# A two-layer decoder trunk on one core: more weight chunks in seven block products, and later stores of the residual

## The chip, the cores and the metric

The kernel runs on one core of one Trainium2 chip. The metric is the device time of one execution in microseconds (us), lower is better. Before the change the median of three executions is 2463.84 us (2461.32 to 2466.27).

The engines are named as in the profile: PE is TensorE's matmul, PEld its loading of the stationary operand, DVE is VectorE, ACT is ScalarE, POOL is GpSimd, SP is SyncE, which here only issues DMAs.

## The reference

Input and output are float32, 256 positions by 2048 channels, two layers. Cut to what matters:

```python
for l in range(2):
    h = rms_norm(x, mix_norm[l])
    proj = h @ w_in[l]                       # 2048 x 7680: q, k, v, u, v of the gating unit, two gates
    branch_a = sliding_window_attention(...) @ w_attn_branch[l]     # 1024 x 2048
    branch_b = chunked_sgu(...) @ w_sgu_branch[l]                   # 1024 x 2048
    x = x + (sigmoid(gate_a) * branch_a + sigmoid(gate_b) * branch_b) @ w_out[l]      # 2048 x 2048
    h2 = rms_norm(x, ffn_norm[l])
    x = x + (silu(h2 @ w_gate[l]) * (h2 @ w_up[l])) @ w_down[l]     # 2048 x 5632 twice, 5632 x 2048
```

All weights are float32 and are read from HBM once.

## The kernel before

**Split products.** A float32 product is made of three matmuls (lines 399 to 401): every operand is split into a high part and the rest, and high by high, high by low and low by high are summed in PSUM. For a weight piece of 128 partitions by 1024 elements ACT makes the high part (`whi`, line 256) and DVE the rest (`wlo`, line 264). The activations are kept in "units": 512 channels, transposed, split into `uh` and `ul`.

**Jobs and parts.** The work is a list of jobs; a job is one product of all units with 1024 columns of a weight (a pair of 512-column chunks; `g6` stands below for the gate columns of the pair of chunks 6 and 7, `u6` for the up columns of that pair, `d0` and `d2` for the two column halves of the down projection). A unit of a job is either *whole*, in four parts of 12 matmuls each (48 matmuls, 4 weight pieces to split), or in *seven products* (the 2 by 2 block scheme that saves one block product of eight): 42 matmuls, but 7 pieces to split and 4 block sums more, which DVE makes out of the raw weights (line 240: `sum<-raw`, `raw<-raw,raw`, `raw<-raw,sum`, `sum<-raw,raw`). Each of these DVE instructions works on 128 x 1024 elements. The number of units of a job in seven products is its `m`; they stand at the job's head, and the tail of their products is mixed with the whole parts behind them. For seven products the units need sums of their own activations too (`sh`, `sl`); for these the first two units of the gate and up jobs have them already, since the gate jobs have `m` = 2.

**What sets the order.** Everything is in a fixed order, written by the program: no engine is scheduled freely. `Stream` runs ahead of PE: the low parts up to five pieces ahead (`N_LOW` = 5 buffers), the high parts six, the raw weights in five buffers of 1 MB (`N_RAW`). A block sum is emitted at a place counted in parts from the head of its job (`SUM_AT`): for `m` = 2 five to six of the eight stand among the last parts of the job before, since DVE works ahead. Loads go out on SP's queue, in order, each when DVE has split the last piece of the buffer that it takes. `tick` counts slots, 0.5 for a product and 1 for a whole part; `after(n, fn)` puts work n slots later. After each job its accumulators are evicted: ACT for gate columns (`silu`, line 1088), DVE for up columns (line 1094) and for the residual (lines 995 and 997).

**Transposing.** A new unit is transposed in blocks: DVE transposes 32 x 32 blocks (`blk`, line 483), sixteen small DMAs issued by POOL bring them into place (`tt`, line 489), ACT scales (line 583, where there is a norm) and splits (`uh`, lines 511 and 587), DVE makes the rest (`ul`, lines 508 and 590). A unit with sums has DVE make and ACT split these as well (lines 520, 523, 508).

**The residual.** It lies in HBM (`kept0` to `kept3`, 512 KB each) between its uses. `fetch_x` (line 356) brings a quarter in, `added` adds the accumulators, and `keep_x` (line 359) stores it, 7 or 8 slots after the end of its column chunk, on SP's queue. This happens behind the output projection (where the quarters also become the units of the next norm, and so are transposed while the first gate job `g0` runs) and behind each of the three rounds of the feed-forward part.

**Rounds.** The 11 chunks of the feed-forward part go in three rounds (0 to 3, 4 to 7, 8 to 10): gate pair, up pair, gate pair, up pair, then the down projection of these chunks. Chunk 10 has no partner; its gate and up columns form one job, `gu10`.

```python
M_OUT, M_FFN, M_DOWN = (0, 1), (2, 1, 1), 1
...
                    for w, m in zip((w_gate, w_up), M_FFN if f else (1, 1)):
```

So before the change every gate pair but the first has two units of four in seven products, every other job of the feed-forward part one.

Of the kernel before, what the change touches and what calls it, by code (L numbers as in the profile page):

```python
# [37 lines left out]
N_BIG = 25  # L38
G_BUSY, G_LAND = 3.5, 3
T1_LATE, THEN_LATE, UNIT_LATE = (1.5, 3), (3, 7), (3, 3)  # L40
Q_FIRST = 15
Q_STEP = 4
LOAD_BY = (1, 2, 3, 4)
ROUNDS = ((0, 1, 2, 3), (4, 5, 6, 7), (8, 9, 10))
M_OUT, M_FFN, M_DOWN = (0, 1), (2, 1, 1), 1
M_Q = 0
M_GATE, M_ATT, M_SGU = (1, 1, 1, 1), (0, 0), (1, 0)
M_V, M_U = 1, 1
# [4 lines left out]
def hybrid_trunk(ctx: ExitStack, tc: tile.TileContext, x, mix_norm, w_in, q_norm, k_norm, sinks,  # L53
# [106 lines left out]
    for l in range(DEPTH):  # L160
        wl = w_in[l]
        for o in (0, None)[::-1 if l == 0 else 1]:
            add_job([wl[:, o:o + CW2]], m=M_Q * l) if o is not None else add_job([wl[:, O_KV:O_KV + CW]])
        for o, m in ((O_V, M_V), (O_U, M_U), (O_GATE, M_GATE[0]), (O_GATE + CW2, M_GATE[1])):
            add_job([wl[:, o:o + CW2]], m=m)
        add_job([wl[:, O_GATE + D:O_GATE + D + CW2]], m=M_GATE[2])
        for i, o in enumerate((0, CW2)):
            add_job([w_attn_branch[l, :, o:o + CW2]], m=M_ATT[i])
        add_job([wl[:, O_GATE + D + CW2:O_GATE + 2 * D]], m=M_GATE[3])
        for i, o in enumerate((0, CW2)):  # L170
            add_job([w_sgu_branch[l, :, o:o + CW2]], m=M_SGU[i])
        for i, o in enumerate((0, CW2)):
            add_job([w_out[l, :, o:o + CW2]], m=M_OUT[i])
        for fs in ROUNDS:
            for f in fs[::2]:
                if f + 1 < NF:
                    for w, m in zip((w_gate, w_up), M_FFN if f else (1, 1)):
                        add_job([w[l, :, f * CW:(f + 2) * CW]], m=m)
                else:
                    add_job([w[l, :, f * CW:(f + 1) * CW] for w in (w_gate, w_up)], m=M_FFN[2])  # L180
            for o in (0, CW2):
                add_job([w_down[l, :, o:o + CW2]], units=list(fs), m=M_DOWN)

    needed = {}
    for i, n in uses:
# [109 lines left out]
    def after(n, fn):  # L295
        steps.append((slot_no[0] + n, fn))
# [61 lines left out]
    def keep_x(c):  # L358
        nc.sync.dma_start(rows(kept[c]), xt[c])
        home[c] = kept[c]  # L360
# [608 lines left out]
    def residual(units, nxt, sums, out_at=None, scale=None):  # L969

        for j in range(0, NCH, 2):

            def done(c, ps, j=j):
                o = j + c

                square_at = 5 if c == 0 else behind(2, 2, 5)

                def then():
                    nxt.unit(o, sums=o < sums)
                    after(square_at, lambda: nxt.squares(o))  # L980
                    if o == NCH - 1:
                        after(square_at + 1, lambda: nxt.finish())

                evicting(c, lambda t: added(o, t, ps), then if nxt is not None else None, late_then=UNIT_LATE)
                if out_at is None:
                    after(7 if c == 0 else 8, lambda: keep_x(o))

            def added(o, t, ps):
                n = 2 if out_at is not None and o == NCH - 1 else 1
                w = CW // n  # L990
                for i in range(n):
                    sl = slice(i * w, (i + 1) * w)
                    d, src = xt[o][:, t, sl], ps[t][:, sl]
                    if scale is None:
                        nc.vector.tensor_tensor(out=d, in0=src, in1=d, op=ALU.add)  # L995
                    else:
                        nc.vector.scalar_tensor_tensor(out=d, in0=src, scalar=scale, in1=d, op0=ALU.mult, op1=ALU.add)  # L997
                    if out_at is not None:
                        eng = nc.sync if i == 0 else nc.scalar
                        eng.dma_start(out_at[0, t * P:(t + 1) * P, o * CW + i * w:o * CW + (i + 1) * w], d)  # L1000

            job = jobs[job_no[0]]
            length = 3.5 * job.m + 4 * (len(job.units) - job.m)
            after(length - 8, lambda j=j: fetch_x(j))
            after(length - 6, lambda j=j: fetch_x(j + 1))
            run(units, done)
# [3 lines left out]
    for l in range(DEPTH):  # L1010

        pl = layer[l]
        parameters(pl)
        kv = slot([P, NT, CW], name="kv")
        qs = [slot([P, NT, CW], name="q") for _ in range(2)]
        att, spa = Attention(pl), Spatial(pl, norm)

        def scaled_into(c, dst, ps):
            evicting(c, lambda t: None,
                     ahead=lambda t: nc.scalar.activation(dst[:, t, :], ps[t], AF.Copy, scale=norm.r[t]))  # L1020

        def kv_done(c, ps):
            scaled_into(0, kv, ps)
            att.keys(kv)
            if l:
                att.begin()

        def q_done(c, ps):
            scaled_into(c, qs[c], ps)
            att.queries(c, qs[c])  # L1030
            if c == 1 and not l:
                att.begin()

        after(2, lambda unit=norm.units[0]: add_sums(unit))
        for done in (kv_done, q_done)[::-1 if l else 1]:
            run(norm.units, done)
        run(norm.units, spa.v)
        run(norm.units, spa.u)

        ga, gb, mT = [None] * NCH, [None] * NCH, [None] * NCH  # L1040

        def gate(dst, j):
            def done(c, ps):
                dst[j + c] = slot([P, NT, CW], name="gate")
                def tanh(t):
                    nc.scalar.activation(dst[j + c][:, t, :], ps[t], AF.Tanh, scale=norm.rh[t])

                evicting(c, lambda t: None, ahead=tanh)
            run(norm.units, done)

        def branch(dst, j, units, then=None):
            def done(c, ps):
                d = dst[j + c]

                def then_():
                    then(j + c)
                    transposed(mT, j + c, ga[j + c], sums=j + c == 0)

                evicting(c, lambda t: nc.vector.scalar_tensor_tensor(out=d[:, t, :], in0=d[:, t, :], scalar=1.0,
                                                                     in1=ps[t], op0=ALU.add, op1=ALU.mult),  # L1060
                         then_ if then is not None else None)
            run(units, done)

        def merge(j):
            nc.vector.tensor_tensor(out=flat(ga[j]), in0=flat(ga[j]), in1=flat(gb[j]), op=ALU.add)

        for j in (0, 2):
            gate(ga, j)
        gate(gb, 0)
        for j in (0, 2):  # L1070
            branch(ga, j, att.attT)
        after(SGU_SUMS, lambda unit=spa.sguT[0]: add_sums(unit))
        gate(gb, 2)
        for j in (0, 2):
            branch(gb, j, spa.sguT, merge)

        norm = Norm(ffn_cols(l))
        residual(mT, norm, max(M_FFN), scale=0.5)

        nxt = Norm(mix_cols(l + 1)) if l + 1 < DEPTH else None  # L1080
        for i, fs in enumerate(ROUNDS):
            hid, hT = {}, {}

            def gate_done(f, c, ps):
                hid[f] = a = slot([P, NT, CW], name="hid")

                evicting(c, lambda t: None,
                         ahead=lambda t: nc.scalar.activation(a[:, t, :], ps[t], AF.Silu, scale=norm.r[t]))

            def up_done(f, c, ps):  # L1090
                a = hid[f]

                def upped(t):
                    nc.vector.scalar_tensor_tensor(out=a[:, t, :], in0=ps[t], scalar=norm.r[t], in1=a[:, t, :],
                                                   op0=ALU.mult, op1=ALU.mult)

                evicting(c, upped, lambda: transposed(hT, f, a, on_pe=f == NF - 1, sums=f in fs[:M_DOWN]))

            for f in fs[::2]:
                if f + 1 < NF:  # L1100
                    run(norm.units, lambda c, ps: gate_done(f + c, c, ps))
                    run(norm.units, lambda c, ps: up_done(f + c, c, ps))
                else:
                    run(norm.units, lambda c, ps: (gate_done, up_done)[c](f, c, ps))
            if i == len(ROUNDS) - 1:
                if nxt is not None:
                    prepare(l + 1)
                residual(hT, nxt, M_Q, out if nxt is None else None)
            else:
                residual(hT, None, 0)  # L1110
        norm = nxt
# [37 lines left out]
```

## Time and profile before

| | us |
|---|---|
| median of three executions | 2463.84 |
| the profiled execution, its own time | 2466.55 |
| its span, first to last instruction | 2464.6 |
| PE busy | 2443.4 (99%) |
| DVE busy | 1990.1 (81%) |
| ACT busy | 1429.3 (58%) |
| POOL busy | 475.0 (19%) |

Read the share of a job, not of the span, since DVE's share differs from job to job. A matmul's row lasts 0.39 us though the next one starts 0.23 us later, since matmuls are pipelined: what one costs is read from start to start. Times in rows count from the start of the span.

### The profile page before, as it was taken

How to read it: one execution, taken by the hardware profiler on the slowest of the kernel's cores; microseconds unless marked ns; L12 is line 12 of the kernel's file. 1: busy time of each engine (PE TensorE's matmuls, PEld its weight loads, DVE VectorE, ACT ScalarE, POOL GpSimd, SP SyncE). 2: the span in 40 equal slices, each digit the busy share in tenths (PEclk: the TensorE clock that was granted, in tenths of full speed). 3: DMA queues.
4: the chain of work that ended last, by engine and by line, in shares of the span. 5: the costliest groups of instructions: out<-in, count | busy, mean ns of one | idle time of the engine just before them, and what ended most of it. 6: DMA issues, size and time to landing. Idle time of an engine off the chain costs nothing. (4 is left out here: it accounts for less than half of the span.)

```text
span 2464.6 us, 30889 instructions
## 1 busy us (share of the span) xinstructions
PE 2443.4 (99%) x10950; PEld 2012.3 (82%) x10950; DVE 1990.1 (81%) x2189; ACT 1429.3 (58%) x1758; POOL 475.0 (19%) x903
## 2 busy tenths in 40 slices
PE   9999999999999999999999999999999999999999
PEld 7888888877888888888888888887778888888887
DVE  7898768786978797788879976777869787978786
ACT  6575545475655665465666665554756555655653
POOL 1421300441220022002235022014402200220020
PEclk9999999999999999999999999999999999999999
DMA  8555556776576757666776546566856757575764
GB/s 311 195 202 190 165 188 218 225 251 216 213 242 205 256 197 243 226 248 198 267 262 218 184 165 201 190 202 205 284 197 222 239 194 263 209 238 190 260 205 166
DMA packets 179051, 539.20 MB, mean 219 GB/s; under 512 B 23872, under 2 KB 26544, under 8 KB 178896
## 3 DMA queue, kind: packets, MB, share of 16 engines
q1 hardware_dynamic: 150832, 508.51, 60.5%
q0 software_dynamic: 27744, 28.44, 3.8%
q8 instruction: 86, 1.41, 0.2%
q14 instruction: 69, 0.57, 0.1%
q10 hardware_dynamic: 320, 0.27, 0.0%
HBM read 492.04 MB, written 16.78 MB: 206 GB/s over the span
## 5 line engine op out<-in xcount | busy, mean ns | idle before, releaser
L264 DVE TENSOR_TENSOR wlo<-raw,whi 128x1024 fp32r<-128x1024 f32 (+1 forms) x956 | 1150.5, 1219 | 381.6 <-PE acc L400 278.6
L256 ACT ACTIVATE whi<-raw 128x1024 fp32r<-128x1024 f32 (+1 forms) x956 | 997.2, 1057 | 692.8 <-PE acc L401 611.9
L399 PE MATMUL acc<-whi,uh 128*128 128x512 f32 x3004 | 1178.0, 392 | 6.8 <-ACT uh L587 4.2
L400 PE MATMUL acc<-wlo,uh 128*128 128x512 f32 x3004 | 1171.1, 390 | 2.4 <-DVE wlo L264 2.4
L401 PE MATMUL acc<-whi,ul 128*128 128x512 f32 x3004 | 1171.7, 390 | 1.4 <-DVE ul L590 1.2
L489 POOL DMA_DIRECT2D tt<-blk x800 | 392.1, 497 | 1682.6 <-DVE blk L483 665.4
L399 PEld LDWEIGHTS acc<-whi,uh 128*128 128x128 f32 x3004 | 565.1, 188 | 128.9 <-ACT uh L587 5.5
L401 PEld LDWEIGHTS acc<-whi,ul 128*128 128x128 f32 x3004 | 565.0, 188 | 121.4 <-DVE ul L590 3.3
L400 PEld LDWEIGHTS acc<-wlo,uh 128*128 128x128 f32 x3004 | 565.2, 188 | 119.8 <-DVE wlo L264 4.0
L399 PE MATMUL acc<-whi,sh 128*128 128x512 f32 x464 | 182.4, 393 | 2.8 <-ACT acc L435 2.2
L256 ACT ACTIVATE whi<-sum 128x1024 fp32r<-128x1024 f32 x116 | 122.8, 1058 | 102.1 <-PE acc L401 87.0
L400 PE MATMUL acc<-wlo,sh 128*128 128x512 f32 x464 | 181.6, 391 | 0.0
L401 PE MATMUL acc<-whi,sl 128*128 128x512 f32 x464 | 181.4, 391 | 0.0
L264 DVE TENSOR_TENSOR wlo<-sum,whi 128x1024 fp32r<-128x1024 f32 x116 | 141.3, 1218 | 6.1 <-PE acc L400 6.1
L399 PEld LDWEIGHTS acc<-whi,sh 128*128 128x128 f32 x464 | 87.5, 188 | 25.7 <-ACT acc L435 6.6
L435 ACT ACTIVATE acc<-acc 128x512 f32<-128x512 f32 x150 | 88.4, 589 | 28.7 <-PE acc L401 20.2
L401 PEld LDWEIGHTS acc<-whi,sl 128*128 128x128 f32 x464 | 87.5, 189 | 18.4
L400 PEld LDWEIGHTS acc<-wlo,sh 128*128 128x128 f32 x464 | 87.5, 189 | 18.0 <-DVE wlo L264 0.3
L590 DVE TENSOR_TENSOR ul<-tt,uh 128x1024 fp32r<-128x1024 f32 x36 | 44.0, 1223 | 42.8 <-ACT uh L587 37.6
L240 DVE TENSOR_TENSOR raw<-raw,sum 128x1024 f32<-128x1024 f32 x58 | 71.0, 1225 | 2.0
L240 DVE TENSOR_TENSOR sum<-raw,raw 128x1024 f32<-128x1024 f32 x58 | 71.0, 1224 | 1.4
L240 DVE TENSOR_TENSOR sum<-raw 128x1024 f32<-128x1024 f32 x58 | 70.7, 1219 | 0.0
(126 smaller groups left out, 1044.5 us busy)
## 6 DMA issues: line engine op xcount, KB each, us to landing
raw<-in_w_in_dram SPq DMA_DIRECT2D x112, 1024.0 KB, 5.5
raw<-in_w_down_dram SPq DMA_DIRECT2D x88, 1024.0 KB, 6.3
raw<-in_w_gate_dram SPq DMA_DIRECT2D x80, 1024.0 KB, 6.3
raw<-in_w_up_dram SPq DMA_DIRECT2D x80, 1024.0 KB, 6.4
raw<-in_w_out_dram SPq DMA_DIRECT2D x32, 1024.0 KB, 6.9
tt<-blk POOLq DMA_DIRECT2D x800, 32.0 KB, 4.9
raw<-in_w_attn_branch_dram SPq DMA_DIRECT2D x16, 1024.0 KB, 6.0
raw<-in_w_sgu_branch_dram SPq DMA_DIRECT2D x16, 1024.0 KB, 5.7
```

What stands on the lines that cost most here:

```text
L240: nc.vector.tensor_tensor(out=self.raw(dst), in0=self.raw(one), in1=self.raw(two), op=ALU.subtract)
L256: nc.scalar.activation(hi[:, k, :], raw[:, k, :], AF.Copy)
L264: nc.vector.tensor_tensor(out=lo[:, k, :], in0=raw[:, k, :], in1=hi[:, k, :].bitcast(F32), op=ALU.subtract)
L399: nc.tensor.matmul(ps, a, hi, start=first, stop=False, skip_group_check=True)
L400: nc.tensor.matmul(ps, a, lo, start=False, stop=False, skip_group_check=True)
L401: nc.tensor.matmul(ps, b, hi, start=False, stop=last, skip_group_check=True)
L435: nc.scalar.activation({"11": x, "t2": e, "t3": y}[name], a, AF.Copy)
L489: nc.gpsimd.dma_start(blocks(d)[:, :, i] if whole else d[:, i].rearrange("p k t c -> p (k t) c"), src)
L590: nc.vector.tensor_tensor(out=blocks(unit.lo), in0=tv, in1=blocks(unit.hi).bitcast(F32), op=ALU.subtract)
```

## The change

Two things are changed. First, `m` of five jobs in each layer goes from 1 to 2: of the up jobs of chunk pairs 2, 4, 6 and 8, and of `gu10`. The up pair of chunks 0 and 1 stays at 1, and so do the down jobs (their new table holds 1 everywhere). Second, where the residual's quarters become units of a norm (behind the output projection, and behind the last round of the first layer), they are stored 20 slots after the end of their columns instead of 7 or 8.

```diff
+KEEP_LATE = 20
...
-M_OUT, M_FFN, M_DOWN = (0, 1), (2, 1, 1), 1
+M_OUT, M_FFN, M_DOWN = (0, 1), (2, 2, 2), ((1, 1), (1, 1), (1, 1))
+UP_TWO = (2, 4, 6, 8)
...
-        for fs in ROUNDS:
+        for fs, ms in zip(ROUNDS, M_DOWN):
             for f in fs[::2]:
                 if f + 1 < NF:
-                    for w, m in zip((w_gate, w_up), M_FFN if f else (1, 1)):
+                    for w, m in ((w_gate, M_FFN[0] if f else 1), (w_up, M_FFN[1] if f in UP_TWO else 1)):
                         add_job([w[l, :, f * CW:(f + 2) * CW]], m=m)
                 else:
                     add_job([w[l, :, f * CW:(f + 1) * CW] for w in (w_gate, w_up)], m=M_FFN[2])
-            for o in (0, CW2):
-                add_job([w_down[l, :, o:o + CW2]], units=list(fs), m=M_DOWN)
+            for o, m in zip((0, CW2), ms):
+                add_job([w_down[l, :, o:o + CW2]], units=list(fs), m=m)
...
                 if out_at is None:
-                    after(7 if c == 0 else 8, lambda: keep_x(o))
+                    after(KEEP_LATE if nxt is not None else 7 if c == 0 else 8, lambda: keep_x(o))
```

In the whole program PE has 10502 rows where it had 10562: 60 matmuls less, six for each of the ten units.

The order of DVE around the head of `u6` in the first layer, before. Rows with `wlo` are the pieces of this job in the order in which PE takes them, first the piece of the first product; line 240 makes the block sums, and line 590 the low part of a transposed hidden unit:

```order
L264 TENSOR_TENSOR wlo_7551<-raw_7383,whi_7530 128x1024
L240 TENSOR_TENSOR raw_7383<-raw_7396,sum_7520 128x2x512
L264 TENSOR_TENSOR wlo_7568<-sum_7520,whi_7549 128x1024
L240 TENSOR_TENSOR sum_7520<-raw_7396,raw_7383 128x1024
L264 TENSOR_TENSOR wlo_7588<-raw_7383,whi_7566 128x1024
L264 TENSOR_TENSOR wlo_7605<-raw_7396,whi_7586 128x1024
L590 TENSOR_TENSOR ul_7445<-tt_7446,uh_7444 128x1024
L264 TENSOR_TENSOR wlo_7629<-raw_7383,whi_7603 128x1024
```

The same place in the changed kernel, again from the piece of the first product on (line 266 is the former 264, 242 the former 240, 592 the former 590):

```order
L266 TENSOR_TENSOR wlo_7575<-raw_7405,whi_7553 128x1024
L242 TENSOR_TENSOR raw_7405<-raw_7418,sum_7525 128x2x512
L266 TENSOR_TENSOR wlo_7592<-raw_7492,whi_7573 128x1024
L242 TENSOR_TENSOR raw_7492<-raw_7545,sum_7557 128x2x512
L266 TENSOR_TENSOR wlo_7612<-sum_7525,whi_7590 128x1024
L266 TENSOR_TENSOR wlo_7629<-sum_7557,whi_7610 128x1024
L242 TENSOR_TENSOR raw_7492<-raw_7545,raw_7492 128x2x512
L592 TENSOR_TENSOR ul_7467<-tt_7468,uh_7466 128x1024
L266 TENSOR_TENSOR wlo_7654<-raw_7405,whi_7627 128x1024
L242 TENSOR_TENSOR sum_7525<-raw_7418,raw_7405 128x1024
L266 TENSOR_TENSOR wlo_7665<-raw_7492,whi_7652 128x1024
L242 TENSOR_TENSOR sum_7557<-raw_7545,raw_7492 128x1024
```

Between the low part of the first product and that of the seventh (`wlo_7677`, the row after the last one shown) there are now twelve steps of DVE, of which five are block sums. One block sum more than before (`sum_7557<-raw_7492`) also stands ahead of the first row.

SP's queue behind the output projection of the first layer, before, from the second load for `g0` on (line 220 loads weights, 356 fetches and 359 stores a quarter of the residual):

```order
L220 DMA raw_4412<-in_w_gate_dram 128x2x1024
L359 DMA kept_100<-x_4101 128x2x512
L220 DMA raw_4456<-in_w_gate_dram 128x2x1024
L356 DMA x_4471<-in_x_dram 128x2x512
L359 DMA kept_101<-x_4136 128x2x512
L356 DMA x_4511<-in_x_dram 128x2x512
L220 DMA raw_4523<-in_w_gate_dram 128x2x1024
```

And in the changed kernel, from the third load for `g0` on (lines 222, 358 and 361):

```order
L222 DMA raw_4455<-in_w_gate_dram 128x2x1024
L358 DMA x_4470<-in_x_dram 128x2x512
L358 DMA x_4509<-in_x_dram 128x2x512
L222 DMA raw_4521<-in_w_gate_dram 128x2x1024
L222 DMA raw_4542<-in_w_gate_dram 128x2x1024
L222 DMA raw_4664<-in_w_gate_dram 128x2x1024
L222 DMA raw_4678<-in_w_gate_dram 128x2x1024
L222 DMA raw_4714<-in_w_gate_dram 128x2x1024
L361 DMA kept_100<-x_4101 128x2x512
L222 DMA raw_4762<-in_w_up_dram 128x2x1024
L361 DMA kept_101<-x_4136 128x2x512
L222 DMA raw_4795<-in_w_up_dram 128x2x1024
```

The first two stores now stand around the first load for `u0`, and the other two, formerly there, follow the last load for `u0`.

2 lines of the change are left out of this document (1 added, 1 removed).

## The prediction

> **What bounds the kernel now.** I read the page's busy table first, then its groups, then PE's waits, then stretches job by job.
>
> ```profile
> span 2464.6 us, 30889 instructions
> PE 2443.4 (99%) x10950; PEld 2012.3 (82%) x10950; DVE 1990.1 (81%) x2189; ACT 1429.3 (58%) x1758; POOL 475.0 (19%) x903
> ...
> L264 DVE TENSOR_TENSOR wlo<-raw,whi 128x1024 fp32r<-128x1024 f32 (+1 forms) x956 | 1150.5, 1219 | 381.6 <-PE acc L400 278.6 <-ACT whi L256 57.6 <-issue 30.6
> ```
>
> PE is hardly idle, and what DVE waits for is mostly PE (278.6 us until a matmul frees a `wlo` buffer). So PE sets the time, and DVE is the engine with the least room. PE's own waits, the three longest:
>
> ```profile
> PE acc L399 <- ACT uh L587: 4.2, 2, 2.2
> PE acc L400 <- DVE wlo L264: 2.4, 4, 0.8
> PE acc L399 <- ACT acc L435: 2.2, 3, 1.0
> ```
>
> That is little, 8.8 of 2464.6 us; but stretch by stretch (span; then PE, PEld, DVE, ACT, POOL busy; granted clock; DMA share; GB/s) the jobs differ:
>
> ```profile
> 535.10:586.20 51.10, 46.72 (x188) 36.80 (x187) 38.89 (x44) 31.97 (x45) 17.54 (x34) 0.93 0.62 206
> 795.80:836.60 40.80, 40.80 (x182) 33.78 (x181) 35.00 (x32) 26.12 (x28) 0.00 (x0) 1.00 0.61 232
> 836.60:878.80 42.20, 42.20 (x187) 34.83 (x186) 32.83 (x31) 22.68 (x25) 1.33 (x3) 1.00 0.58 201
> 878.80:919.60 40.80, 40.80 (x181) 33.80 (x180) 40.70 (x42) 28.39 (x31) 14.30 (x30) 1.00 0.64 231
> 919.60:961.80 42.20, 42.20 (x187) 34.82 (x186) 31.61 (x30) 22.69 (x25) 1.05 (x3) 1.00 0.59 200
> 1759.00:1810.50 51.50, 46.91 (x188) 36.49 (x188) 39.34 (x45) 31.90 (x45) 17.44 (x34) 0.93 0.61 204
> ```
>
> These are `g0`, `g4`, `u4`, `g6` and `u6` of the first layer, and `g0` of the second. A feed-forward job with one unit in seven products takes 42.2 us, one with two (`g4`, `g6`) 40.8, with PE busy throughout, though in `g6` DVE is at 40.70 of 40.80. The two `g0` hold the work of a 42.2 us job and take 51.1 and 51.5: 18.2 us are lost there, at a clock of 0.93.
>
> **Part 1: ten more units in seven products.** This removes 60 matmuls. What one costs is the step from start to start:
>
> ```profile
> 569.29 0.39 PE L399 MATMUL acc<-whi,uh 128*128 128x512 f32 x1
> ...
> 570.42 0.39 PE L401 MATMUL acc<-whi,ul 128*128 128x512 f32 x1
> 572.82 0.50 PE L399 MATMUL acc<-whi,uh 128*128 128x512 f32 x1 [2.01 <-ACT uh L587]
> ...
> 574.08 0.79 PE L401 MATMUL acc<-whi,ul 128*128 128x512 f32 x1 [0.53 <-DVE ul L590]
> 574.67 0.63 PE L399 MATMUL acc<-whi,uh 128*128 128x512 f32 x1
> 575.10 0.63 PE L400 MATMUL acc<-wlo,uh 128*128 128x512 f32 x1
> ```
>
> From the first to the second row are five steps: (570.42 − 569.29) / 5 = 0.226 us, and 60 × 0.226 = **13.6 us** less. The step from 42.2 to 40.8, 1.4 for each unit, says the same.
>
> The Trainium skill (TensorE: Matmul & The Clock Gate, Back-to-back issue gap) gives some 131 ns for a pair of weight load and 512-column matmul in a long stream. By it, as an estimate, 60 pairs save 7.9 us; here the starts lie 226 ns apart, so the trace disagrees and the measurement decides.
>
> Each unit adds three `wlo` and four block sums on DVE and three `whi` on ACT. DVE's rows at the end of `g6`:
>
> ```profile
> 907.21 1.22 DVE L264 TENSOR_TENSOR wlo<-raw,whi 128x1024 fp32r<-128x1024 f32 x1
> ...
> 911.75 1.22 DVE L264 TENSOR_TENSOR wlo<-raw,whi 128x1024 fp32r<-128x1024 f32 x1
> 913.00 1.23 DVE L240 TENSOR_TENSOR raw<-raw,sum 128x1024 f32<-128x1024 f32 x1
> ```
>
> From the first to the second row are four steps, 4.54 us: queued, they start 1.14 us apart, so seven more are 8.0 us: `u6` would have 31.6 + 8.0 = 39.6 us of DVE work in 40.8, `u4` 40.8 in 40.8. `u4`, `g6` and `u6` together come to 32.8 + 40.7 + 31.6 + 16.0 = 121.1 in 122.4. It fits on average. What decides is a job's head, where a product takes PE 6 × 0.226 = 1.36 us, and DVE 1.14 for its piece and as much for each block sum beside it.
>
> PE starts `u6` at 919.6 and needs the first low piece one matmul later, at 919.8. It is ready at 911.75 + 1.22 = 912.97, 6.9 us ahead. In the new order one more block sum stands before it: 5.7 ahead. From it to the piece of the seventh product are twelve steps, 12 × 1.14 = 13.7, against 6 × 1.36 = 8.2 of PE: 0.2 us ahead. The pieces behind have no sums between them and gain on PE again. Neighbours that depend on each other start up to 1.25 apart (911.75 to 913.00), which eats the 0.2, so I put 0.25 us of wait on each of four such heads (`u2` and `u6`, both layers): **1.0 us**. `u4` and `u8` follow jobs in which DVE has room (35.00 of 40.80), and `gu10` follows `u8` as `g6` follows `u4`, with the same transposing; I put nothing on them.
>
> ACT's three `whi` raise `u6` from 22.7 us to some 26 of 40.8, and that room hides them; without it they would delay `wlo`, at the same kind of wait. The loads are the same, but sooner needed:
>
> ```profile
> raw<-in_w_up_dram SPq DMA_DIRECT2D x80, 1024.0 KB, 6.4
> ```
>
> The fourth buffer of `u6` is freed by the piece at 907.21, in the new order at about 909.6, and first read six steps later, 6.8 us against 6.4 to land: hidden, just. Bounds of part 1: below, no wait, 13.6 gained. Above, all four heads lose what the worst wait of the trace cost (572.82 is 2.2 us late, 574.08 0.7 more, then some ten matmuls at 0.43: 5 us): 20 − 13.6 = 6.4 lost. I take 12.6 gained, since `g6` runs without a wait at full DVE.
>
> **Part 2: the stores.** `g0` loses time at two places. At its head (543.09) PE waits for ACT's copy of an accumulator, and this for DVE, which is behind: it and ACT, both in order, had stood in the job before until the second quarter's transposing DMAs landed (522.39), and have worked without a pause since. Later the last quarter's unit is late (572.82). In turn: PE at the head; ACT's waits on the second to the fourth quarter; POOL's last issues for the third and the fourth; SP's stores; and the DMA traffic from 500 to 527:
>
> ```profile
> 543.09 0.67 PE L399 MATMUL acc<-whi,sh 128*128 128x512 f32 x1 [0.98 <-ACT acc L435]
> ```
>
> ```profile
> 522.39 1.71 ACT L583 ACTIVATE tt<-tt,vcols 128x256 f32<-128x256 f32 x4 [4.16 <-DMA tt<-blk]
> ...
> 555.25 1.71 ACT L583 ACTIVATE tt<-tt,vcols 128x256 f32<-128x256 f32 x4 [1.15 <-DMA tt<-blk]
> ...
> 569.97 1.71 ACT L583 ACTIVATE tt<-tt,vcols 128x256 f32<-128x256 f32 x4 [6.22 <-DMA tt<-blk]
> ```
>
> ```profile
> 547.50 2.03 POOL L489 DMA_DIRECT2D tt<-blk  x4 [1.48 <-DMA tt<-blk]
> ...
> 561.85 0.98 POOL L489 DMA_DIRECT2D tt<-blk  x2 [0.49 <-DMA tt<-blk]
> ```
>
> ```profile
> 552.18 2.64 SPq L220 DMA_DIRECT2D raw<-in_w_up_dram  x2
> 554.87 0.46 SPq L359 DMA_DIRECT2D kept<-x  x1
> ...
> 560.89 0.46 SPq L359 DMA_DIRECT2D kept<-x  x1
> ```
>
> ```profile
> DMA packets 3700, 9.61 MB, mean 356 GB/s; under 512 B 623, under 2 KB 623, under 8 KB 3698
> ```
>
> In that last stretch the first two stores are issued. At 356 GB/s their 1 MB takes 2.9 us of the same 16 DMA engines that carry the small DMAs; without them ACT's 4.16 would be some 1.3. The third quarter's DMAs, with no store beside them, landed 5.7 us after their last issue (549.53 to 555.25), the fourth's, with two, 7.1 (562.83 to 569.97). The change takes the stores from both places. But the first two now follow the last load for `g0`, around the first of the two loads that SP issues here between 552.18 and 554.82: beside the end of the third quarter's DMAs and the start of the fourth's. The third quarter's split (1.71 us of scaling, then a `uh` and a `ul` of 1.06 and 1.22) ends some 4 us after 555.25. PE takes that unit after seven products and four whole parts, 7 × 1.36 + 4 × 2.71 = 20.4 us from the head at 536, and the 3 to 4 us lost at the head: about 560. So there is under 1 us to spare, and a later landing of the third quarter would be paid. Queued on SP behind the moved stores are the loads for `u0`; the stores wait for nothing by then (their additions are a job old), so these are not held up beyond the 0.46 us of an issue, and each quarter's buffer gets its next tile a job later.
>
> Of the 18.2 us some 5 in each layer hang on the fourth quarter (2.2 + 0.7 + the slow matmuls), the other 4 on the head. For the fourth quarter I take 3 of 5 in each layer: it lands 1.4 us sooner by the tails, the rest stays late, but with a shorter gap and a shorter slow stretch behind it. For the head 3 of 4 in the first layer, where ACT's wait is the cause by its size, and 0.5 in the second, where I see no row that ties the head to a store. For the new place I give back 1.5: 6 + 3.5 − 1.5 = **8 us**. The stores at the end of the first layer move too; PE's list of waits names no long one of that place, and I put nothing there. Bounds: 18 gained; 6 lost, if two quarters more land 1.5 us late in each layer.
>
> **The sum.** −13.6 + 1.0 − 8 = −20.6, so the profiled execution (2466.55, span 2464.6) becomes 2446. It lay 2.7 over the median of 2463.84; against that, **2443 us**.
>
> **Rivals.**
> - *The stores were not what made the small DMAs late; the loads are.* Two stores are 1.05 of the 9.61 MB in the stretch shown, loads most of the rest. For it: that share. Against: 5.7 beside 7.1. Part 2 then gives nothing: 2463.8 − 12.6 = 2451. (The Trainium skill, DMA: Bandwidth & Descriptors, Queues, rings and completion order, says each DMA engine takes the queues that have work in turn, packet by packet. By that rule a longer line of stores on SP's queue takes nothing from POOL's while loads fill it anyway, which is this rival; the 7.1 speaks against it.)
> - *The stores collide at their new place.* Two quarters land later; the head gains 3.5, but 3 per layer are lost and the fourth quarter gains nothing: 2463.8 − 12.6 − 3.5 + 6 = 2454.
> - *DVE does not hold the heads (slower).* Where the twelve steps run over PE's clock by more than about 2 us, PE stops and resumes at 0.43 a matmul, some 5 us a head as at 572.82. At four heads that is 20, which ends near 2463.8 − 13.6 + 20 − 8 = 2462; at all ten, 50, at 2492. It is slower from six heads on. Against it: `g6`, and 0.2 us ahead by the rows.
>
> **Chances.** Forecast 0.55, no gain from the stores 0.25, collision 0.1, DVE not holding 0.1 (half of it slower). A measurement of this kernel tells about 0.2% (4.9 us) from no change. The first three all lie below 2458.9: faster 0.89; same 0.06, slower 0.05. Range 2434 (16 us from the stores, no wait at heads) to 2457 (past the collision); the forecast's own is 2436 to 2449.
>
> **What would show it.** Right: up jobs and `gu10` of 40.8 us with PE busy throughout and DVE near full; PE with 60 matmuls less; `g0` at 45 to 48 us; ACT's waits on `tt` under 3 us there. Wrong: PE waits on `wlo` at the heads of `u2` or `u6` above 1 us, a granted clock under 1 there; `g0` still at 51, or waits on the third quarter's `uh`.

## The result and the profile after

The changed kernel takes 2446.86 us (median, 2445.43 to 2447.69) beside 2463.39 for the kernel before: 16.5 us less, a ratio of 0.9931 (95% interval 0.9914 to 0.9949). In a second comparison it takes 2446.32 beside 2465.78, a ratio of 0.9917 (0.9904 to 0.9931). The forecast was 2443.

The page of the changed kernel, the busy table and the largest group of DVE:

```profile
span 2446.0 us, 30959 instructions
PE 2424.5 (99%) x10890; PEld 1996.9 (82%) x10890; DVE 2061.7 (84%) x2259; ACT 1461.0 (60%) x1788; POOL 477.2 (20%) x903
...
L266 DVE TENSOR_TENSOR wlo<-raw,whi 128x1024 fp32r<-128x1024 f32 (+1 forms) x966 | 1157.7, 1218 | 288.4 <-PE acc L402 190.3
```

PE has 60 matmuls less (10950 to 10890), DVE 70 instructions and 72 us more, and what DVE waited for PE has shrunk from 278.6 us to 190.3. DVE has less room, and PE is still the engine that is hardly ever idle.

Stretch by stretch, with the columns as in the prediction: `g0` of the first layer, `g4`, `u4`, `g6` and `u6`, then `g0` of the second layer.

```profile
535.10:582.00 46.90, 43.99 (x188) 34.48 (x187) 38.40 (x45) 31.21 (x44) 17.05 (x34) 1.00 0.66 225
790.30:831.10 40.80, 40.80 (x182) 33.80 (x181) 37.26 (x34) 26.13 (x28) 0.00 (x0) 1.00 0.61 232
831.10:871.90 40.80, 40.80 (x182) 33.80 (x181) 38.04 (x36) 25.80 (x28) 1.38 (x3) 1.00 0.56 208
871.90:912.70 40.80, 40.80 (x182) 33.80 (x181) 40.70 (x42) 28.73 (x31) 14.30 (x30) 1.00 0.64 231
912.70:953.70 41.00, 41.00 (x182) 33.73 (x181) 38.61 (x38) 25.90 (x28) 1.15 (x3) 1.00 0.56 206
1747.50:1798.40 50.90, 44.24 (x188) 34.40 (x187) 40.19 (x45) 32.72 (x46) 17.03 (x34) 1.00 0.60 207
```

`u4` and `u6` now take 40.80 and 41.00 instead of 42.2. `g0` of the first layer went from 51.1 to 46.9, that of the second only from 51.5 to 50.9. Cut by job (the first matmul of each job to that of the next), the difference of the two spans, 18.6 us, is made up of 13.8 in the ten jobs that got a second unit in seven products, 4.3 in the first `g0`, 0.6 in the second, and less than 0.8 up or down in any other job.

PE's waits in the changed kernel, the first three of the list:

```profile
PE acc L401 <- ACT uh L589: 2.7, 3, 2.3
PE acc L402 <- DVE wlo L266: 2.2, 4, 0.7
PE acc L401 <- ACT acc L437: 2.2, 3, 1.0
```

The wait on `uh` was 4.2 us in two large pieces, both for the last quarter's unit, and is 2.7 now, 2.3 of it in one piece. That one is in the second layer. Here are the two places, PE's rows at the last quarter's unit in the first layer and in the second, and ACT's rows ahead of them:

```profile
570.10 0.50 PE L401 MATMUL acc<-whi,uh 128*128 128x512 f32 x1 [0.22 <-ACT uh L589]
...
1786.55 0.50 PE L401 MATMUL acc<-whi,uh 128*128 128x512 f32 x1 [2.27 <-ACT uh L589]
```

```profile
567.25 1.71 ACT L585 ACTIVATE tt<-tt,vcols 128x256 f32<-128x256 f32 x4 [4.42 <-DMA tt<-blk]
...
1783.70 1.70 ACT L585 ACTIVATE tt<-tt,vcols 128x256 f32<-128x256 f32 x4 [6.49 <-DMA tt<-blk]
```

In the first layer the quarter is 0.2 us late, in the second still 2.3. The `ul` of the same unit costs another 0.7 at each place, just behind.

### The profile page after: what moved, and what is told of

Its sections match the earlier page's. It is cut to its first block, busy times and chain, and to the rows that moved or that the text cites. A ratio compares the mean times of both kernels' runs of the same rounds, so it can differ in the third digit from the quotient of the medians.

```text
span 2446.0 us, 30959 instructions
## 1 busy us (share of the span) xinstructions
PE 2424.5 (99%) x10890; PEld 1996.9 (82%) x10890; DVE 2061.7 (84%) x2259; ACT 1461.0 (60%) x1788; POOL 477.2 (20%) x903
## 5 line engine op out<-in xcount | busy, mean ns | idle before, releaser
L266 DVE TENSOR_TENSOR wlo<-raw,whi 128x1024 fp32r<-128x1024 f32 (+1 forms) x966 | 1157.7, 1218 | 288.4 <-PE acc L402 190.3
L401 PE MATMUL acc<-whi,uh 128*128 128x512 f32 x2904 | 1137.4, 392 | 5.2 <-ACT uh L589 2.7
L403 PE MATMUL acc<-whi,ul 128*128 128x512 f32 x2904 | 1131.1, 390 | 2.3 <-DVE ul L592 2.1
L402 PE MATMUL acc<-wlo,uh 128*128 128x512 f32 x2904 | 1131.1, 389 | 2.2 <-DVE wlo L266 2.2
L401 PEld LDWEIGHTS acc<-whi,uh 128*128 128x128 f32 x2904 | 545.3, 188 | 123.0 <-ACT uh L589 4.4
L401 PE MATMUL acc<-whi,sh 128*128 128x512 f32 x544 | 212.6, 391 | 3.6 <-ACT acc L437 2.2
L258 ACT ACTIVATE whi<-sum 128x1024 fp32r<-128x1024 f32 x136 | 143.9, 1058 | 118.1 <-PE acc L403 99.5
L402 PE MATMUL acc<-wlo,sh 128*128 128x512 f32 x544 | 212.0, 390 | 0.0
L403 PE MATMUL acc<-whi,sl 128*128 128x512 f32 x544 | 211.8, 389 | 0.0
L266 DVE TENSOR_TENSOR wlo<-sum,whi 128x1024 fp32r<-128x1024 f32 x136 | 165.1, 1217 | 11.1 <-PE acc L402 10.2
L242 DVE TENSOR_TENSOR raw<-raw,raw 128x1024 f32<-128x1024 f32 x68 | 82.8, 1218 | 0.0
```

Of the source, the lines that this page charges most:

```text
L242: nc.vector.tensor_tensor(out=self.raw(dst), in0=self.raw(one), in1=self.raw(two), op=ALU.subtract)
L258: nc.scalar.activation(hi[:, k, :], raw[:, k, :], AF.Copy)
L266: nc.vector.tensor_tensor(out=lo[:, k, :], in0=raw[:, k, :], in1=hi[:, k, :].bitcast(F32), op=ALU.subtract)
L401: nc.tensor.matmul(ps, a, hi, start=first, stop=False, skip_group_check=True)
L402: nc.tensor.matmul(ps, a, lo, start=False, stop=False, skip_group_check=True)
L403: nc.tensor.matmul(ps, b, hi, start=False, stop=last, skip_group_check=True)
```

## The experiments

Every ratio is to the kernel before, timed in the same comparison. Profiles show one execution of each kernel. The theory was that the two parts add up, that the seven products are worth what their matmuls take, and that the stores are what makes the last quarter late. The main rival was that the loads alone do that, or that the shorter `g0` came from chance.

### Each part alone

Part 1 alone:

```diff
-                    after(KEEP_LATE if nxt is not None else 7 if c == 0 else 8, lambda: keep_x(o))
+                    after(7 if c == 0 else 8, lambda: keep_x(o))
```

> The ten units in seven products alone; the stores stay where they were before the change. Theory (the two parts add up): the ten jobs lose 13.8 us between them as in the profile of the changed kernel, both g0 stay at about 51 us (51.1 and 51.5 before), so 2463.4 - 13.5 = about 2450. Rival (the shorter g0 of the first layer, 46.9 us, is not the stores but a stretch of half clock that happened to be absent in that one execution): g0 of the first layer comes out at 47 to 48 here too, and the time at about 2446 to 2447, as the changed kernel.

Measured: 2451.69 (2447.47 to 2457.82), ratio 0.9951 (0.9936 to 0.9965): 12.6 us less by the medians, 12.1 by the ratio, near the 12.6 forecast for it, with the widest spread of all runs. The profiled execution was the fastest one (2447.47), and in it the two `g0` took 48.1 and 49.4 us, not 51: the last quarter's unit was late by 1.1 and 1.0 us there. So this profile alone does not exclude chance, and where the other four executions lost 2.3 to 10.4 us more is not seen; what speaks against chance are the medians and the next runs.

Part 2 alone:

```diff
+KEEP_LATE = 20
...
-                    after(7 if c == 0 else 8, lambda: keep_x(o))
+                    after(KEEP_LATE if nxt is not None else 7 if c == 0 else 8, lambda: keep_x(o))
```

> The later stores alone, with the old numbers of units in seven products. Theory (the stores shorten g0 of the first layer by 4.3 us and that of the second by 0.6, as in the profile of the changed kernel): about 2463.4 - 5 = 2458.5, g0 at 47 and 51. Rival (stores do not matter, half clock comes and goes): 2463, g0 at 51 in both layers in the profile or at a mixture. Prediction's own size: 2463.4 - 8 = 2455.

Measured: 2459.83 (2456.95 to 2461.99), ratio 0.9980 (0.9971 to 0.9989): 4.4 us less by the medians, 4.9 by the ratio, where the forecast had 8. The two parts together, 12.1 and 4.9, are 17.0, and the change gives 17.0 by its first ratio and 20.5 by its second. Each of these has an interval of 2 to 4 us either way, so they add up as far as the runs can tell.

### Are the stores the cause, and is 20 slots late enough?

```diff
-KEEP_LATE = 20
+KEEP_LATE = 28
```

> The changed kernel with the stores 28 slots late instead of 20: the first two then follow the fourth and the fifth load for u0, after the last of the fourth quarter's small DMAs is issued; nothing is stored while the third and fourth quarters are brought into place. Theory (the stores lengthen SP's line of loads, and the small DMAs land when that line has drained): the fourth quarter's DMAs land 4.5 to 5 us after their last issue in both layers (4.7 and 6.7 now), the wait of 2.44 us in the second layer's g0 falls under 0.6, and the time goes to 2446.9 - 2.5 = about 2444. Rival (the loads alone do it): 6 to 7 us after the last issue in the second layer as now, g0 there at 51, time 2447.

Measured: 2442.23 (2440.62 to 2442.74), 4.1 to 4.6 us less than the changed kernel's two medians. The second layer first, ACT's rows of the last two quarters and SP's queue beside them:

```profile
1764.90 1.71 ACT L585 ACTIVATE tt<-tt,vcols 128x256 f32<-128x256 f32 x4 [2.17 <-DMA tt<-blk]
...
1776.67 1.71 ACT L585 ACTIVATE tt<-tt,vcols 128x256 f32<-128x256 f32 x4 [3.99 <-DMA tt<-blk]
```

```profile
1762.39 13.41 SPq L222 DMA_DIRECT2D raw<-in_w_up_dram  x4
1775.85 0.46 SPq L361 DMA_DIRECT2D kept<-x  x1
```

and the same part of SP's queue in the changed kernel:

```profile
1765.90 0.37 SPq L222 DMA_DIRECT2D raw<-in_w_up_dram  x1
1766.32 1.11 SPq L361 DMA_DIRECT2D kept<-x  x1
1768.17 21.11 SPq L222 DMA_DIRECT2D raw<-in_w_up_dram  x4
```

With 28 slots the stores go out behind the fourth load for `u0`. ACT waits 3.99 us for the last quarter instead of 6.49, and PE has no wait on its `uh` any more, in either layer. The two `g0` take 44.8 and 47.3 us. With 20 slots both stores stand ahead of the loads that are under way while the last quarter's small DMAs are, the second of them in the row at 1766.32.

Then the stores were left out altogether:

```diff
-                if out_at is None:
-                    after(KEEP_LATE if nxt is not None else 7 if c == 0 else 8, lambda: keep_x(o))
+                if out_at is None and nxt is None:
+                    after(7 if c == 0 else 8, lambda: keep_x(o))
```

> The changed kernel without the stores behind the two output projections and behind the last round of the first layer: these 12 stores of 512 KB are left out (later fetches then read older values, with as many bytes). This takes the suspected cost away altogether. Theory (stores): g0 at 46 to 47 us in both layers, as with the stores 28 slots late or up to 1 us better, 2443 to 2444. Rival (loads alone): g0 of the second layer at 50 to 51 as in the changed kernel, time 2446 to 2447.

Measured: 2441.7 (2439.72 to 2443.04), the two `g0` 44.6 and 47.2: no better than with 28 slots beyond 0.5 us, which the spread of either run covers. So the stores at their old place cost 2451.7 − 2441.7 = 10.0 us in all, give or take 5 by the two intervals, mostly because of the spread of part 1 alone; 20 slots win back about half, 28 slots nearly everything. The rival that the loads alone do it has fallen. What these runs also show is what the stores do not do. PE's waits at the head of the second layer's `g0`, without any store:

```profile
1748.12 0.47 PE L401 MATMUL acc<-whi,sh 128*128 128x512 f32 x1 [1.66 <-DVE x L999]
1752.08 0.50 PE L402 MATMUL acc<-wlo,uh 128*128 128x512 f32 x1 [0.73 <-DVE wlo L266]
1754.49 0.50 PE L401 MATMUL acc<-whi,sh 128*128 128x512 f32 x1 [0.98 <-ACT acc L437]
```

The same 0.98 on ACT's copy of an accumulator stood in the profile of before. Most of the head's waits are there without any store; what they hang on is read below, where the prediction is answered.

### What holds the head of `g0`

Two runs on top of the 28 slots. First the fifth up job of each layer, then also `g0` with no unit in seven products:

```diff
-UP_TWO = (2, 4, 6, 8)
+UP_TWO = (0, 2, 4, 6, 8)
```

> The changed kernel with the stores 28 slots late, and with two units in seven products in the fifth up job of each layer too, that of chunks 0 and 1. 12 matmuls less are 12 x 0.2267 = 2.7 us. Theory (DVE holds on average, its work in u0, g2 and u2 is then about 41 + 40.7 + 38.6 = 120 of 122.4 us): 2442.2 - 2.7 + at most 0.7 of waits = about 2440. Rival (three full jobs behind one another are too much: u0 leaves g2 with a smaller lead, and g2 and u2 wait for low parts, 1 to 3 us a layer): 2442 to 2446.

Measured: 2439.70 (2438.67 to 2441.27), 2.5 us less than with 28 slots alone. `u0` takes 40.80 in both layers, and so does the `g2` behind it. DVE holds three full jobs behind one another; the `u2` behind them takes 40.97 and 41.62 us.

```diff
-                    for w, m in ((w_gate, M_FFN[0] if f else 1), (w_up, M_FFN[1] if f in UP_TWO else 1)):
+                    for w, m in ((w_gate, M_FFN[0] if f else 0), (w_up, M_FFN[1] if f in UP_TWO else 1)):
```

> As the run with the fifth up job, and with no unit in seven products in g0: against the stores 28 slots late alone as many matmuls (g0 48 + 48 + 48 + 48, u0 42 + 42 + 48 + 48). It takes seven DVE steps of 1.14 us, 8 us, from where DVE is behind at the head of g0. Theory (what is left at the head of g0, 1.15 us in the first layer and 1.5 + 0.9 + 1.15 in the second, is this backlog): 1 to 2.5 us less in each layer, minus 0.5 for u0: 2442.2 - 3 = about 2439. Rival (the head waits for evictions, which stay): 2442 to 2443.

Measured: **2434.24** (2432.99 to 2434.36), ratio 0.9876 (0.9861 to 0.9891): 8 us less than with 28 slots alone, at the same number of matmuls, where the theory had 3. This is the fastest kernel of the study, 12.6 us under the changed one. Its two `g0`:

```profile
535.50:579.00 43.50, 43.50 (x194) 36.03 (x193) 32.51 (x35) 27.56 (x38) 16.80 (x34) 1.00 0.66 218
1742.20:1786.70 44.50, 43.79 (x194) 35.92 (x193) 34.35 (x38) 27.44 (x38) 16.79 (x34) 1.00 0.68 228
```

PE is busy throughout in the first, 192 × 0.2267 = 43.5 us, and DVE has 32.5 us of work there instead of 37.6. From start to start, beyond 0.2267 us a matmul, the heads of the two `g0` lose 1.0 us where they lost 5.4 with 28 slots alone, and the third and fourth quarters nothing where they lost 2.3. The gain was larger than forecast since more moved than DVE's seven steps: in front of a job without a unit in seven products the last accumulator is evicted half a slot sooner, and the fourth quarter's transposing is called after two slots instead of three (DVE ended its blocks at 541.2 instead of 549.6), so the `ul` of a quarter was not late either. The two causes were not tried apart.

### How near DVE is to its end

```diff
+    twice = set()
...
+                        head = len(parts)
                         add_job([w[l, :, f * CW:(f + 2) * CW]], m=m)
+                        if w is w_up and f in (2, 6):
+                            twice.update(i for i in sums if sums[i][0] == head <= i)
...
-            nc.vector.tensor_tensor(out=self.raw(dst), in0=self.raw(one), in1=self.raw(two), op=ALU.subtract)
+            for _ in range(2 if i in twice else 1):
+                nc.vector.tensor_tensor(out=self.raw(dst), in0=self.raw(one), in1=self.raw(two), op=ALU.subtract)
```

> The stores 28 slots late, and the first of the two last block sums of u2 and u6 made twice in a row, in both layers: one DVE step of 1.14 us more at four heads, with the same results. It prices the step at which the forecast saw PE and DVE level (0.05 us of lead in the profile of the changed kernel). Theory (no lead is left there): each of the four jobs 1.14 us longer, 41.0 to 42.1, all others unchanged: 2442.2 + 4.6 = about 2447. Rival (the waits are made up for by other reserves): under 1 us in all, 2442 to 2443. If a wait of 1.3 us is followed by a stretch of matmuls at half clock, up to 5 us for each such head, 2447 to 2462.

Measured: 2446.97 (2445.76 to 2448.89), 4.7 us more than with 28 slots. The stretches of `u2` and `u6` in the first layer:

```profile
665.00:707.20 42.20, 41.38 (x181) 33.63 (x181) 39.89 (x38) 26.13 (x28) 1.06 (x3) 1.00 0.54 199
914.00:956.20 42.20, 41.38 (x182) 33.62 (x181) 39.81 (x38) 27.30 (x30) 1.12 (x3) 1.00 0.55 200
```

42.2 instead of 41.0 us: one step more on DVE at this place is paid in full. It was paid in waits of under 1 us, and no slow matmuls followed them.

### Whether it is the queue

The changed kernel with its 20 slots, and the stores on ACT's queue:

```diff
-        nc.sync.dma_start(rows(kept[c]), xt[c])
+        nc.scalar.dma_start(rows(kept[c]), xt[c])
```

> The changed kernel (20 slots) with every store of the residual issued on ACT's queue instead of SP's. Theory (what counts is that 1 MB more of bytes goes over the same 16 DMA engines while the small DMAs are under way, from whichever queue): as the changed kernel, 2446 to 2448. Rival one (SP's line is what counts, a store on another queue does not lengthen it): as the run with 28 slots, 2442 to 2443. Rival two (queues are served in turn, so a third busy queue takes from POOL's share): the third or fourth quarter lands 1 to 3 us later than in the changed kernel, 2448 to 2453.

Measured: 2442.91 (2442.70 to 2444.14), as with 28 slots on SP's queue. The last quarter's DMAs landed 4.6 and 5.1 us after their last issue, and PE did not wait for its `uh`; in the first layer it was the third quarter's unit that came 0.8 us late instead. But ACT also issued the first two stores of the first layer at 545.23 and 549.11 instead of 547.48 and 552.13, so a last run set the number of slots to 21 to bring these times together:

> As the run with the stores on ACT's queue, 21 slots late instead of 20: ACT then issues the first two behind g0's output projection at about 547.5 and 552.4 us, the times at which SP issued them in the changed kernel (547.48 and 552.13), where ACT with 20 slots issued them at 545.23 and 549.11. It tells apart why ACT's queue was 4 us cheaper. Theory (the 2.3 to 3 us by which the stores went out sooner is what helped; the bytes count, not the queue): 2446 to 2447, the fourth quarter late again. Rival (the queue is what helps: a store on ACT's queue does not lengthen SP's line of loads): 2442.5 to 2443.5 as with 20 slots.

Measured: 2442.86 (2441.48 to 2443.47). It does not tell the two apart: ACT's order moved with it, and the stores were issued at 543.96 and 547.99, sooner still and not later. Whether the queue or the earlier time helps stays open. The Trainium skill (DMA: Bandwidth & Descriptors, Queues, rings and completion order) says that a DMA engine serves its queues in turn; by that alone a third busy queue should take from the small DMAs, 2448 or more, and both runs lie 5 us below.

### Whether a spare 4 us hides the stores

The fastest kernel with its stores at 7 and 8 slots again:

```diff
-                    after(KEEP_LATE if nxt is not None else 7 if c == 0 else 8, lambda: keep_x(o))
+                    after(7 if c == 0 else 8, lambda: keep_x(o))
```

> The run with no unit in seven products in g0 and two in u0, but with the stores back at 7 and 8 slots, where they were before the change. In its run with 28 slots the fourth quarter's DMAs landed 559.2 us into the span and the split of that quarter ended at about 563.5, while PE asks for it some 32.6 us after the start of g0, at 567.5: 4 us to spare that the other kernels do not have. Theory (the stores cost time only while the fourth quarter is on the path): about the 2434.2 of the run with 28 slots, at most 2436. Rival (the stores cost the same wherever, 9.5 us between 7 slots and 28 slots as between 2451.7 and 2442.2): 2442 to 2444.

Measured: 2439.86 (2438.76 to 2443.15), 5.6 us more than with 28 slots: between the two theories, so the 4 us do not hide them. In the first layer the fourth quarter is late after all, which costs 2.1 us. POOL's queue shows what had been left out, here the early stores, then the 28 slots, for the end of the fourth quarter's issues:

```profile
552.02 4.01 POOL L491 DMA_DIRECT2D tt<-blk  x8 [1.67 <-DMA tt<-blk]
558.72 1.47 POOL L491 DMA_DIRECT2D tt<-blk  x3 [2.68 <-DMA tt<-blk]
```

```profile
551.01 3.92 POOL L491 DMA_DIRECT2D tt<-blk  x8 [0.99 <-DMA tt<-blk]
556.20 0.50 POOL L491 DMA_DIRECT2D tt<-blk  x1 [1.27 <-DMA tt<-blk]
```

POOL itself waits for earlier small DMAs before it can issue the next ones. The trace shows why: the program gives these DMAs eight semaphores in turn, and each waits until the one eight before it has landed (the issue at 558.72 for that of 552.02, which landed at 558.44). A store beside them is paid twice, in the landing and in the issue: from the end of DVE's blocks to the landing of the last DMA the fourth quarter took 24.0 us with early stores and 18.0 with late ones.

In the second layer it took 20.6 and 19.0, and the fourth quarter was in time with either. There the loss is at the head of `g0`, 4.1 us instead of 1.0, of which 1.6 are slow matmuls behind one longer wait: the second quarter's small DMAs had landed later. ACT's row of that quarter and PE's wait, with early stores, then with 28 slots:

```profile
1735.16 1.71 ACT L585 ACTIVATE tt<-tt,vcols 128x256 f32<-128x256 f32 x4 [4.56 <-DMA tt<-blk]
```

```profile
1751.54 0.50 PE L401 MATMUL acc<-whi,uh 128*128 128x512 f32 x1 [2.13 <-DVE x L999]
```

```profile
1730.74 1.71 ACT L585 ACTIVATE tt<-tt,vcols 128x256 f32<-128x256 f32 x4 [3.56 <-DMA tt<-blk]
```

```profile
1747.11 0.50 PE L401 MATMUL acc<-whi,uh 128*128 128x512 f32 x1 [0.71 <-DVE x L999]
```

### Second profiles of both kernels

> The kernel before, once more, for a second profile. Theory (the stretches of matmuls at half clock, which cost about 6 of the 18.2 us lost in the two g0 of the first profile, come in one execution and stay away in another after the same wait): the waits at the head of g0 (about 0.9 and 1.15 us) and at the fourth quarter (1 to 2.4 us) come again, the half clock behind them does not at all three places; g0 between 47.5 and 51. Rival (half clock follows by rule on a wait of over 1 us): the same stretches at the same places, 51.1 and 51.5.

One more execution of the kernel before (2465.95 us): the two `g0` take 50.5 and 50.5. At the head of the first there are the same waits (0.9 and 1.15), but now no slow matmuls behind them. At the fourth quarter the waits are 2.9 and 2.2 us, and slow matmuls follow both.

> The changed kernel, once more, timed beside the others of this call, for a second profile. Theory: 2446.9 again within 1.5 us; g0 of the first layer 46.9 within 1, that of the second 49 to 51, with the fourth quarter's unit 1 to 2.5 us late in the second layer. Rival (the second layer's late quarter was chance): g0 47 in both, 2443.

The changed kernel: 2446.32 (2443.63 to 2447.35). The first `g0` takes 47.3 and the second 48.8; the last quarter's unit is 1.4 and 0.9 us late. So the split between the layers in the first profile (0.2 and 2.3) was that execution's; that the quarter is late by 2 to 3 us in both layers together is what comes again.

## Why the prediction was right or wrong

**The sum.** −20.6 was forecast; −16.5 and −19.5 by the medians were measured in two comparisons. The direction, the order of the two parts and the range held. Part 1 came as summed. Part 2 alone was worth 4.4 to 4.9 us where 8 were forecast, and the term that failed is the head of `g0`. The table shows what PE lost in the two `g0` together, from start to start beyond 0.2267 us a matmul (us; the head is all up to the third quarter's matmuls). The first four columns are the two profiles of each kernel.

| | before | before, second | changed | changed, second | 28 slots | no stores |
|---|---|---|---|---|---|---|
| head | 7.3 | 5.4 | 6.3 | 6.0 | 5.4 | 5.3 |
| third quarter | 0.5 | 1.6 | 2.4 | 1.5 | 1.3 | 1.5 |
| fourth quarter | 10.4 | 9.7 | 4.7 | 4.2 | 1.0 | 0.7 |

The forecast had −3.5, +1.5 and −6 for the three rows; the first pair of profiles gives −1.1, +2.0 and −5.7, the second +0.6, 0.0 and −5.5. The terms:

- *60 matmuls, −13.6.* Right. Part 1 alone gives 12.1 to 12.6 with its waits, the ten jobs 13.8 in the profile (one of them had lost 0.5 before for another reason). The 0.2267 us from start to start is what a matmul cost.
- *Four heads at 0.25 us, +1.0.* Right in place and nearly in size: `u2` and `u6` took 40.97 to 41.00 instead of 40.80, 0.7 in all. DVE's rows at the head of `u6`, from the piece of the first product to that of the seventh, and PE's two matmuls that need them:

```profile
905.93 1.22 DVE L266 TENSOR_TENSOR wlo<-raw,whi 128x1024 fp32r<-128x1024 f32 x1
...
919.81 2.35 DVE L266 TENSOR_TENSOR wlo<-raw,whi 128x1024 fp32r<-128x1024 f32 x2
```

```profile
912.89 0.39 PE L402 MATMUL acc<-wlo,uh 128*128 128x512 f32 x1
...
921.08 0.50 PE L402 MATMUL acc<-wlo,uh 128*128 128x512 f32 x1
```

  The first piece is ready at 905.93 + 1.22 = 907.15, 5.7 us ahead, as counted. The seventh's is ready at 919.81 + 1.22 = 921.03, 0.05 ahead of a matmul that already came 0.02 later than the step; PE lost 0.17 there. `u4`, `u8` and `gu10` lost nothing. The rival in which DVE does not hold was 0.05 us away at two jobs of each layer: one more DVE step there costs 1.14 us at once.
- *The fourth quarter, −6.* Right in size, and so is the cause, the stores: with them 28 slots late, or left out, the quarter loses 1.0 us or less in the two layers together. It landed sooner by the tails (from the last issue to the landing) by 2.3, 0.4, 1.0 and 2.0 us in the two layers and two pairs of profiles, on average the 1.4 of the forecast. What is not shown is the path that the forecast had, that the stores' bytes take the 16 DMA engines from the small DMAs: the same bytes on ACT's queue cost nothing that could be measured, but went out sooner.
- *The new place, +1.5.* Costed as a collision with the third quarter. That one loses as much without stores (1.5 us) as with 20 slots in the second profile. The collision that is left is with the fourth quarter, 3 to 4 us against 28 slots. SP's line was longer by these two stores when the loads behind them went out, one of which landed only at 566.0, 12 us after its issue (7.5 with 28 slots). The second rival, a collision at the new place, was half right: 20 slots bring half of the 10 us.
- *The head, −3.5.* This step failed: "without them ACT's 4.16 would be some 1.3". By the profiles the stores make up 0.5 to 1.7 us of ACT's wait for the second quarter's small DMAs in the first layer, not 2.9. Here are ACT's row of that quarter and PE's last wait at the head in the changed kernel, then the same two without stores:

```profile
521.92 1.71 ACT L585 ACTIVATE tt<-tt,vcols 128x256 f32<-128x256 f32 x4 [3.67 <-DMA tt<-blk]
```

```profile
542.62 0.50 PE L401 MATMUL acc<-whi,sh 128*128 128x512 f32 x1 [0.98 <-ACT acc L437]
```

```profile
521.14 1.71 ACT L585 ACTIVATE tt<-tt,vcols 128x256 f32<-128x256 f32 x4 [2.46 <-DMA tt<-blk]
```

```profile
541.84 0.50 PE L401 MATMUL acc<-whi,sh 128*128 128x512 f32 x1 [0.73 <-ACT acc L437]
```

  The chain itself, from this landing over ACT and DVE to PE, was read rightly. From the start of the one row to that of the other it is 20.7 us in both kernels, as before the change (522.39 to 543.09), and in all 24 `g0` of the study that have one unit in seven products; DVE works without a pause in all but the first 2.7 us of it (ACT, which the prediction names beside it, does pause, for 3.17 us ahead of 531.07). So the head is ready a fixed time after the second quarter's landing, and PE waits for whatever of that time is left when it arrives. Without a unit in seven products in `g0` DVE has less to do before it: in the second layer the head lost 1.0 us with ACT's row 11.4 us ahead of `g0`, where 28 slots alone lost 3.9 us with the row 11.5 ahead. In the first layer the head lost, slow matmuls left out, 2.7 and 2.4 us in the two profiles before the change, 2.3 and 1.6 with it, 1.5 with 28 slots and 1.0 without stores. The half clock behind the waits in the first profile, 1.6 us, was chance: the second profile of the kernel before has the waits without it.
- *A term put at nothing.* In the second layer the head lost 3.0 us in both profiles before, 3.1 with part 2 alone, 5.2 with part 1 alone, and 4.0 and 4.4 with both. So the ten units cost 1 us or more there, which is more than the first layer's head gained. Why is open.
- *The rival that the loads make the small DMAs late* has fallen: without the stores the last quarter is in time in both layers, with the same loads.

Of the signs named beforehand the shorter jobs and the 60 matmuls came; `g0` at 45 to 48 us came in the first layer only, and ACT's waits on `tt` in `g0` stayed at 2.2 to 6.5 us, most of them above the 3 that were named.

## What to carry to other kernels

A transfer that nothing waits for is not free while another, small and late, is under way. Ask not only where it stands in its queue but which transfers are still under way behind it, and move it past the last of them (here 28 slots brought nearly all of the 10 us, 20 slots half). A store under way beside a late landing need not be the cause of all its lateness: take the store out before you price it (here ACT's wait of 4.16 us became 2.46, not 1.3). An engine that is busy for nearly all of a job can cost nothing or be paid in full: DVE at 40.70 of 40.80 us cost nothing in `g6`, and at 38.61 of 41.00 in `u6` one more step costs all of its 1.14. Count its steps from the job's head to each point where the fast engine needs them. And where a job's head is crowded, the same saving can be had in the next job: moving one unit in seven products in each layer from `g0` to `u0` kept the number of matmuls and, against the stores 28 slots late, gained 8 us.

## What the runs showed of the hardware

Slow matmuls behind a wait of PE come and go. They start 0.43 us apart instead of 0.23, for 6 to 13 matmuls, and cost 1.4 to 2.9 us in all. The granted clock of such a stretch is lower (0.50 from 1798 to 1802 us in the first profile of the kernel before; over its first `g0` 0.93 there and 0.97 in the second profile; 1.00 in the changed kernel's). In the profiles of this study they followed six of eight waits of 2.2 to 2.9 us at the head or the quarters of `g0`, and four of the many between 0.8 and 2.1. The same wait of 1.15 us at the head of the first `g0` had them in two profiles (the kernel before, and part 1 alone) and not in the others, so the "more than about 2 us" of the prediction is no bound. The Trainium skill (TensorE: Matmul & The Clock Gate, What's actually happening) has the clock halved after an idle window of about 3.4 us, with windows that run freely. That they run freely would fit the coming and going; the waits here were all shorter than 3.4 us, so the length does not agree, and the measurement decides. What decides in a single execution stays open.

A second thing is one of the program and not of the chip, but easily taken for the chip's: since each small DMA waits for the landing of the one eight before it, load beside them lengthens the issuing too. From the blocks to the landing the fourth quarter took 18.0 us and 24.0 with early stores in the first layer, 19.0 and 20.6 in the second. The 6 us of the first layer are for two stores of 512 KB, which take 2.9 us at the 356 GB/s seen before. More semaphores for these DMAs were not tried.
